# The up projection's rows moved by 64 bytes inside their tiles

## The chip, the cores and the metric

The kernel runs on one core of a Trainium2 chip. The metric is the device time of one execution in microseconds: 1368.78 us as the median of three runs before the change. Instructions run on TensorE (PE in the rows; its weight loads are PEld), VectorE (DVE), ScalarE (ACT), GpSimd (POOL) and SyncE (SP), which issues most transfers.

## The reference

Two transformer-like blocks follow each other on 256 tokens of width 1024. The last step of the second block is a mixture of 16,384 tiny experts, and the change touches its second half alone:

```python
def block(args):
    xb, ib, gb = args
    u = w_down[ib]
    act = jax.nn.gelu(jnp.einsum("td,thkd->thk", xb, u), approximate=False) * gb
    v = w_up[ib]
    return jnp.einsum("thk,thkd->td", act, v)
...
return rmsnorm_2(h, norm_final_w)[:, N_META:]
```

Each token takes 8 x 16 experts. The result of the block is added to the stream, and the sum is normed.

## The kernel before, in words

The kernel computes the expert layer densely: for every expert and every token an activation, times a gate that is zero where the token did not choose the expert. The 16,384 experts are 128 rows of 128. The down projection (tile `S`, lines 222 to 224) makes for each row `i` a tile of 128 experts x 256 tokens, `AT`; the up projection multiplies row `i`'s activations with the 128 x 1024 matrix `wu[i]` and adds into four banks of PSUM, `acc[t][f]`, for two halves `t` of the tokens and two halves `f` of the 1024 outputs.

Every product in the kernel is done in two parts for precision. `load_split` (from line 198) loads a 128 x 1024 piece of weights as `wf` (four buffers), ACT casts it to the reduced form `wh` (line 217), and DVE subtracts, `wl = wf - wh` (line 218). The other operand is split in the same way, and three multiplications, high x high, high x low and low x high, take the place of one. In the up projection the function `up_row` (from line 1499) multiplies the row with its gates on DVE (line 1507) and then splits it into `ah` (ACT, line 348) and `al` (DVE, line 349), each 128 x 256 words. Row 0 and row 1 are made earlier (`UP_EARLY`); the rows up to 95 use the pool `gp` and its tags `oh` and `og`, whose slots are as large as the gate tiles of the same tags, 512 words a partition, two of each; from row 96 on a pool `up` with four of each takes their place, in the space that the tile `AT0` of 96 rows leaves.

The inner loop is `products`. Here the row is the stationary operand (128 of its 256 columns, loaded into TensorE by a weight load before every multiplication) and `wu`'s part is the moving one, 512 columns at a time. A row has 2 x 3 x 2 = 12 multiplications, and the 128 rows 1536, in program order; the last three rows do their second half of the tokens at the end. TensorE takes its instructions in the order of the program; loads run ahead on SP's queue as far as the four `wf` buffers allow, and the splits follow them on ACT and DVE.

Where the tiles lie. A tile's place is counted in bytes from a partition's start. `wf`, `wh` and `wl` are 4096 bytes, the slots of `gp` 2048, `AT0` 96 x 1024, the slots of `up` 1024, and `S`'s moving tiles `xth` and `xtl` 8 x 272 words: all are multiples of 256, and in the built program `wh`, `wl`, `ah`, `al`, `xuh` and `xul` all begin 32 bytes past a multiple of 256. So do all slices of `acc`'s operands, which are cut at multiples of 512 bytes. "Distance" below is the moving operand's address minus the stationary operand's, modulo 256. In `acc` it is 0. In the queries' product `q` (moving `xuh`, `xul`, 256 columns) it is 0 as well. In the second feed-forward product (moving `fah`, `fal`, 256 columns), whose tiles lie 224 past a multiple of 256, it is 192 throughout. In `S` (moving `xth`, `xtl`, 256 columns, rows of 272 words) it is 64 x `k` for the eight steps `k`, three multiplications each. The kernel's first projection, `tma` (512 columns) and `tmb` (262 columns), has weights as the moving operand and rows of 272 words as the stationary one, so its distance at step `k` is -64 x `k`: 0 at `k` = 0 and 4, 192 at 1 and 5, 128 at 2 and 6, 64 at 3 and 7.

Of the kernel before, what the change touches and what calls it, by code (L numbers as in the profile page):

```python
# [8 lines left out]
F32R = mybir.dt.float32r  # L9
# [7 lines left out]
P = 128  # L17
T = 256
# [51 lines left out]
LN_WAIT = 1.5, 3.0  # L70

LAST = 3

UP_EARLY = 2

# [83 lines left out]
def tile_two_blocks(ctx: ExitStack, tc: tile.TileContext, A, out):  # L159
# [172 lines left out]
    def pin(ins):  # L332
        tc.keep_in_program_order(ins)
# [11 lines left out]
    def split_to(dh, dl, src, scale=None):  # L345

        if scale is None:
            nc.scalar.copy(dh, src)  # L348
            nc.vector.tensor_sub(dl, src, dh)  # L349
        else:  # L350
            nc.scalar.activation(dh, src, AF.Copy, scale=scale)
            nc.vector.scalar_tensor_tensor(dl, src, scale, dh, op0=OP.mult, op1=OP.subtract)
# [197 lines left out]
    oh = ap.tile([P, 8, T], F32R, name="oh")  # L550
# [298 lines left out]
    for g in range(9):  # L849
# [21 lines left out]
        if g >= 1:  # L871
            ah, al = held[g - 1]
# [356 lines left out]
    for step in ORDER.split():  # L1229
# [28 lines left out]
        elif kind == "w":  # L1258
# [6 lines left out]
            oh, ol = (och, ready["ocl"]) if g >= 8 else pairs[g // 4]  # L1265
            i = g - 8 if g >= 8 else g % 4
# [185 lines left out]
    def at_rows(a, b):  # L1452
        for lo, hi, t in parts:
            x, y = max(a, lo), min(b, hi)
            if x < y:
                yield x, y, t[:, x - lo:y - lo, :]
# [42 lines left out]
    def up_row(i, up):  # L1499

        (_, _, r), = list(at_rows(i, i + 1))
        r = r[:, 0, :]
        n = max(x for x in gts if x <= i)
        gt = gts[n][:, :min(P - n, gts[n].shape[1]), :]
        if i == n and i >= 7:
            pin(nc.sync.dma_start(gt, G0r[:, i:i + gt.shape[1], :]))
        pin(nc.vector.tensor_mul(r[:, :P], r[:, :P], gt[:, i - n, :]))
        ah = up.tile([P, T], F32R, tag="oh", name=f"ah{i}")
        al = up.tile([P, T], F32R, tag="og", name=f"al{i}")
        if i < UP_EARLY:  # L1510
            pin(nc.scalar.copy(ah, r))
            pin(nc.vector.tensor_sub(al, r, ah))
        else:
            split_to(ah, al, r)
        up_rows[i] = (ah, al)

    for i in range(0, P, 2):
        if i == P - 2:

            bg.drain()  # L1520
            for n in (0, 3, 5):
                nc.gpsimd.dma_start(gts[n], G0r[:, n:n + gts[n].shape[1], :])
            for j in range(UP_EARLY):
                up_row(j, gp)
        S = bank(f"S{i}").rearrange("p (a t) -> p a t", a=2)
        for e in range(2):
            wh, wl = load_split(A["wd"][i + e], [P, 8, P])
            for k in range(8):
                mm3(S[:, e, :], wh[:, k, :], wl[:, k, :], xth[:, k, :], xtl[:, k, :], k == 0 and e == 0, k == 7)
            bg.run(BUDGET["select"] if state["toks"] == P else BUDGET["down"])  # L1530
        n = state["toks"]
        rs = list(at_rows(i, i + 2)) if len(parts) > 1 or i < NA else []
        assert len(rs) == 1
        r = rs[0][2]
        if n == P:
            nc.scalar.activation(r, S, AF.Gelu)
        else:
            nc.scalar.activation(r[:, :, :P], S[:, :, :P], AF.Gelu)
            if n < T:
                nc.scalar.activation(r[:, :, n:], S[:, :, n:], AF.Gelu)  # L1540
            g = stage[(i // 2) % 2].rearrange("p (a t) -> p a t", a=2)
            nc.scalar.activation(g[:, :, P:n], S[:, :, P:n], AF.Gelu)
            nc.vector.tensor_mul(r[:, :, P:n], r[:, :, P:n], g[:, :, P:n])
        state["rows"] = i + 2
# [6 lines left out]
    up = gp  # L1551
    for i in range(P):
        if i == NA:

            sat.close()
            up = sp.enter_context(tc.tile_pool(name="up", bufs=4))
        if i == NB:
            pin(nc.scalar.activation(first, first, AF.Sqrt))
        if i not in up_rows:
            up_row(i, up)  # L1560
        ah, al = up_rows.pop(i)
        wh, wl = load_split(A["wu"][i], [P, D])

        def products(t, fs, i=i, ah=ah, al=al, wh=wh, wl=wl):
            c = slice(t * P, (t + 1) * P)
            for l, w, e in ((ah, wh, False), (ah, wl, False), (al, wh, i == P - 1)):
                for f in fs:
                    nc.tensor.matmul(acc[t][f], l[:, c], w[:, f * 512:(f + 1) * 512], start=False, stop=e,  # L1568
                                     skip_group_check=True)

        products(0, (0, 1))
        if i >= P - LAST:
            late.append(products)
        else:
            products(1, (0, 1))
# [109 lines left out]
```

## Time and profile before

| | |
|---|---|
| timed runs | 1365.6, 1368.78 and 1371.24 us |
| profiled execution | 1370.11 us, its span 1368.4 us |
| TensorE busy | 1350.3 us, 99% of the span |
| DVE, ACT, POOL busy | 985.9, 756.3, 307.1 us |
| mean granted clock of TensorE | 0.992 of 2.4 GHz |
| first and last start of a multiplication into `acc` (line 1568) | 1014.3 and 1362.3 us |

The span runs from the first to the last instruction of one profiled execution; the execution's own time holds the start and the end around it too. Matmuls are pipelined and their ends are modelled, so the records of two overlap: what a multiplication costs is read from one start to the next and not from its own length.

### The profile page before, as it was taken

To read this page: it belongs to the slowest core of one execution; us is meant where nothing else is said; L and a number is where in the kernel's file an instruction comes from. 1 tells how busy PE (TensorE), PEld (TensorE's weight loads), DVE (VectorE), ACT (ScalarE), POOL (GpSimd) and SP (SyncE) were. 2 spreads that over 40 slices of the span, in tenths; PEclk is the share of its full clock that TensorE was granted. 3 is DMA by queue.
4 is the path that set the end of the run, shared out by engine and by line. 5 is a ranking of instruction groups with operands and counts; after the bars stand their busy time and mean duration, and the time that the engine had idled before them with its cause. 6 is when DMAs were issued, how large, how long until landed. Compare 5 with 4: busy or idle time off the path is not lost.

```text
span 1368.4 us, 25834 instructions
## 1 busy us (share of the span) xinstructions
PE 1350.3 (99%) x10054; PEld 1255.6 (92%) x10054; DVE 985.9 (72%) x1924; ACT 756.3 (55%) x1263; POOL 307.1 (22%) x223
## 2 busy tenths in 40 slices
PE   9999999999999999999999999999999999999998
PEld 8988899999888899999999999999998888888886
DVE  6985777657637896798989976666666666666665
ACT  6665444445334675654544548787755555555454
POOL 3122200000310000000048888888600000000000
PEclk9999999999999999999999999999999999999999
DMA  8466666663663343645668776666666777677764
GB/s 297 141 220 226 185 185 189 194 189 113 202 195 107 108 141 109 200 143 165 185 184 186 186 186 156 159 151 158 172 201 220 212 224 220 216 218 214 221 210 131
DMA packets 120730, 250.45 MB, mean 183 GB/s; under 512 B 28048, under 2 KB 52368, under 8 KB 120480
## 3 DMA queue, kind: packets, MB, share of 16 engines
q1 hardware_dynamic: 97328, 235.89, 56.3%
q0 software_dynamic: 22704, 12.35, 6.3%
q8 instruction: 79, 1.29, 0.4%
q10 hardware_dynamic: 576, 0.57, 0.1%
q14 instruction: 43, 0.35, 0.1%
HBM read 234.60 MB, written 9.50 MB: 178 GB/s over the span
## 4 chain that ended last, share of the span: by engine, by line
PE 93%; DVE 3%; DMA 2%; ACT 1%; issue 1%; POOL 0%; SPq 0%; DVEq 0%; ACTq 0%; POOLq 0%
PE acc L1568 25%; PE S L224 9%; PE S L223 9%; PE S L222 9%; PE ff L222 4%; PE ff L223 4%; PE ff L224 4%; PE pg L1476 2%; PE cv L922 2%; PE wo L222 2%; PE wo L224 2%; PE wo L223 2%; PE cf L222 1%; PE cf L224 1%; PE cf L223 1%; PE q L223 1%
## 5 line engine op out<-in xcount | busy, mean ns | idle before, releaser
L218 DVE TENSOR_TENSOR wl<-wf,wh 128x1024 fp32r<-128x1024 f32 (+1 forms) x425 | 515.7, 1215 | 234.7 <-ACT wh L217 234.1
L217 ACT CAST wh<-wf 128x1024 fp32r<-128x1024 f32 (+1 forms) x425 | 442.8, 1043 | 377.9 <-PE S L223 145.4
L222 PE MATMUL S<-xth,wh 128*128 128x256 f32 x1024 | 289.6, 283 | 0.0
L223 PE MATMUL S<-xtl,wh 128*128 128x256 f32 x1024 | 288.6, 282 | 0.0
L224 PE MATMUL S<-xth,wl 128*128 128x256 f32 x1024 | 288.3, 282 | 0.0
L1350 POOL DMA_INDIRECT G<-small x128 | 241.9, 1890 | 163.4 <-DVE small L1344 124.7
L224 PEld LDWEIGHTS S<-xth,wl 128*128 128x128 f32 x1024 | 194.2, 190 | 0.0
L222 PEld LDWEIGHTS S<-xth,wh 128*128 128x128 f32 x1024 | 193.8, 189 | 0.0
L223 PEld LDWEIGHTS S<-xtl,wh 128*128 128x128 f32 x1024 | 192.5, 188 | 0.0
L1568 PE MATMUL acc<-wh,ah 128*128 128x512 f32 x512 | 158.3, 389 | 0.0
L1568 PE MATMUL acc<-wl,ah 128*128 128x512 f32 x512 | 158.2, 389 | 0.0
L1568 PE MATMUL acc<-wh,al 128*128 128x512 f32 x512 | 158.1, 389 | 0.0
L348 ACT CAST ah<-AT 128x256 fp32r<-128x256 f32 x126 | 50.9, 404 | 116.4 <-DVE wl L218 114.3
L1568 PEld LDWEIGHTS acc<-wl,ah 128*128 128x128 f32 x512 | 96.2, 188 | 19.9
L1568 PEld LDWEIGHTS acc<-wh,al 128*128 128x128 f32 x512 | 96.2, 188 | 19.8
L1568 PEld LDWEIGHTS acc<-wh,ah 128*128 128x128 f32 x512 | 96.1, 188 | 19.8
L222 PE MATMUL ff<-h2h,wh 128*128 128x256 f32 x256 | 73.1, 287 | 1.0 <-ACT wh L217 0.6
L222 PE MATMUL ff<-fah,wh 128*128 128x256 f32 x256 | 71.3, 280 | 1.7 <-ACT fah L348 1.7
L223 PE MATMUL ff<-h2l,wh 128*128 128x256 f32 x256 | 72.7, 284 | 0.0
L223 PE MATMUL ff<-fal,wh 128*128 128x256 f32 x256 | 71.6, 280 | 1.1 <-DVE fal L349 1.1
L224 PE MATMUL ff<-h2h,wl 128*128 128x256 f32 x256 | 72.2, 284 | 0.4 <-DVE wl L218 0.4
L349 DVE TENSOR_TENSOR al<-AT,ah 128x256 fp32r<-128x256 f32 x126 | 53.4, 424 | 26.2 <-ACT ah L348 26.2
(501 smaller groups left out, 2691.6 us busy)
## 6 DMA issues: line engine op xcount, KB each, us to landing
wf<-in_wd_dram SPq DMA_DIRECT2D x128, 512.0 KB, 3.7
wf<-in_wu_dram SPq DMA_DIRECT2D x128, 512.0 KB, 3.6
wf<-in_w_ff_dram SPq DMA_DIRECT2D x64, 512.0 KB, 4.2
wf<-in_w_out_dram SPq DMA_DIRECT2D x24, 512.0 KB, 3.6
G<-zg POOLq DMA_DIRECT2D x16, 512.0 KB
wf<-in_w_conf_dram SPq DMA_DIRECT2D x16, 512.0 KB, 3.8
wf<-in_w_xbc_dram SPq DMA_DIRECT2D x16, 512.0 KB, 5.0
wf<-in_w_q_dram SPq DMA_DIRECT2D x16, 512.0 KB, 3.7
```

The lines of the kernel that those rows point to most:

```text
L217: nc.scalar.copy(wh[:, :n], wf[:, :n])
L218: nc.vector.tensor_sub(wl[:, :n], wf[:, :n], wh[:, :n])
L222: nc.tensor.matmul(o, lh, rh, start=start, stop=False, skip_group_check=True)
L223: nc.tensor.matmul(o, lh, rl, start=False, stop=False, skip_group_check=True)
L224: nc.tensor.matmul(o, ll, rh, start=False, stop=stop, skip_group_check=True)
L348: nc.scalar.copy(dh, src)
L349: nc.vector.tensor_sub(dl, src, dh)
L922: nc.tensor.matmul(pcv[32 * g:32 * g + 32, i, :], taps[:, m, g, q, :], r4[:, i, g, 4 * q:4 * q + T], start=(i == 0 and q == 0), stop=(q == ...
L1350: s = nc.gpsimd.indirect_dma_start(out=G0, out_offset=bass.IndirectOffsetOnAxis(ap=idx[:, c:c + 1], axis=0), in_=gv[:, c:c + 1], in_offset ...
L1476: nc.tensor.matmul(pg[:, i, :], oh[:, i, :], og[:, i, :], start=True, stop=True, skip_group_check=True)
L1568: nc.tensor.matmul(acc[t][f], l[:, c], w[:, f * 512:(f + 1) * 512], start=False, stop=e, skip_group_check=True)
```

## The change

`UP_PHASE` is a constant of 16 words. Both tiles of a row are allocated 64 words longer, and the row lies from word 16 on. `up_row`, `products` and all else are as before.

```diff
+UP_PHASE = 16
...
-        ah = up.tile([P, T], F32R, tag="oh", name=f"ah{i}")
-        al = up.tile([P, T], F32R, tag="og", name=f"al{i}")
+        ah = up.tile([P, T + 64], F32R, tag="oh", name=f"ah{i}")[:, UP_PHASE:UP_PHASE + T]
+        al = up.tile([P, T + 64], F32R, tag="og", name=f"al{i}")[:, UP_PHASE:UP_PHASE + T]
```

## Rows read from the trace of the kernel before

**Rows 1.** The page: busy time by engine; chain that ended last, by engine and line.
```profile
PE 1350.3 (99%) x10054; PEld 1255.6 (92%) x10054; DVE 985.9 (72%) x1924; ACT 756.3 (55%) x1263; POOL 307.1 (22%) x223
...
PE 93%; DVE 3%; DMA 2%; ACT 1%; issue 1%; POOL 0%; SPq 0%; DVEq 0%; ACTq 0%; POOLq 0%
PE acc L1568 25%; PE S L224 9%; PE S L223 9%; PE S L222 9%; PE ff L222 4%; PE ff L223 4%; PE ff L224 4%; PE pg L1476 2%; PE cv L922 2%; PE wo L222 2%; PE wo L224 2%; PE wo L223 2%; PE cf L222 1%; PE cf L224 1%; PE cf L223 1%; PE q L223 1%
```

**Rows 2.** Busy time by engine, two windows of `acc`; then granted clock, DMA.
```profile
1050.00:1100.00 50.00, 50.00 (x222) 41.45 (x221) 33.78 (x56) 27.26 (x37) 0.00 (x0) 1.00 0.72 218
1100.00:1150.00 50.00, 50.00 (x222) 41.42 (x221) 34.37 (x55) 26.29 (x36) 0.00 (x0) 1.00 0.70 216
```

**Rows 3.** Costs by line, then DMA, 1020 to 1360 us (total us, mean ns).
```profile
L218 DVE TENSOR_TENSOR wl<-wf,wh 128x1024 fp32r<-128x1024 f32 x124 | 152.0, 1226 | 84.3 <-ACT wh L217 84.3
L217 ACT CAST wh<-wf 128x1024 fp32r<-128x1024 f32 x124 | 130.6, 1054 | 42.6 <-issue 39.6 <-PE acc L1568 2.7
...
L349 DVE TENSOR_TENSOR al<-AT,ah 128x256 fp32r<-128x256 f32 x125 | 52.9, 423 | 26.2 <-ACT ah L348 26.2
L348 ACT CAST ah<-AT 128x256 fp32r<-128x256 f32 x125 | 50.5, 404 | 115.5 <-DVE wl L218 114.3 <-issue 1.2
L1507 DVE TENSOR_TENSOR AT<-AT,small 128x128 f32<-128x128 f32 x121 | 34.5, 285 | 0.0
...
DMA packets 33328, 71.60 MB, mean 211 GB/s; under 512 B 2432, under 2 KB 17818, under 8 KB 33306
...
wf<-in_wu_dram SPq DMA_DIRECT2D x120, 512.0 KB, 3.6
```

**Rows 4.** Line 1568: durations min/median/max in ns, first and last start.
```profile
L1568 PE MATMUL acc<-wh,ah x512: 389/389/398, 1014.3 to 1361.8; 128*128 128x512 f32 x171
L1568 PEld LDWEIGHTS acc<-wl,ah x512: 187/188/188, 1014.5 to 1361.8; 128*128 128x128 f32 x171
...
L1568 PE MATMUL acc<-wh,al x512: 387/389/393, 1015.2 to 1362.3; 128*128 128x512 f32 x171
```

**Rows 5.** `fah` from 183 us: weight loads; first and last of 94 timeline rows.
```profile
L222 PEld LDWEIGHTS ff<-fah,wh x30: 187/188/188, 182.9 to 192.7; 128*128 128x128 f32 x30
...
182.65 0.28 PE L222 MATMUL ff<-fah,wh 128*128 128x256 f32 x1
...
193.19 0.28 PE L222 MATMUL ff<-fah,wh 128*128 128x256 f32 x1
```

**Rows 6.** `q` from 579 us: weight loads; first and last of 85 timeline rows.
```profile
L222 PEld LDWEIGHTS q<-xuh,wh x28: 192/192/193, 578.8 to 588.5; 128*128 128x128 f32 x28
...
578.42 0.28 PE L224 MATMUL q<-xuh,wl 128*128 128x256 f32 x1
...
588.50 0.28 PE L224 MATMUL q<-xuh,wl 128*128 128x256 f32 x1
```

**Rows 7.** TensorE's timeline at the beginning of `acc`, two multiplications a row.
```profile
1014.31 0.62 PE L1568 MATMUL acc<-wh,ah 128*128 128x512 f32 x2
1014.76 0.63 PE L1568 MATMUL acc<-wl,ah 128*128 128x512 f32 x2
1015.23 0.62 PE L1568 MATMUL acc<-wh,al 128*128 128x512 f32 x2
1015.69 0.62 PE L1568 MATMUL acc<-wh,ah 128*128 128x512 f32 x2
1016.15 0.63 PE L1568 MATMUL acc<-wl,ah 128*128 128x512 f32 x2
1016.62 0.62 PE L1568 MATMUL acc<-wh,al 128*128 128x512 f32 x2
```

**Rows 8.** Timeline of `S`, first and last of 27 rows.
```profile
639.81 0.28 PE L223 MATMUL S<-xtl,wh 128*128 128x256 f32 x1
...
642.89 0.28 PE L222 MATMUL S<-xth,wh 128*128 128x256 f32 x1
```

**Rows 9.** Timeline of `tma`: at `k` = 4, then at `k` = 5.
```profile
15.22 0.40 PE L222 MATMUL tma<-wh,hh 128*128 128x512 f32 x1
...
15.91 0.28 PE L222 MATMUL tmb<-wh,hh 128*128 128x262 f32 x1
...
18.54 0.39 PE L222 MATMUL tma<-wh,hh 128*128 128x512 f32 x1
...
19.24 0.28 PE L222 MATMUL tmb<-wh,hh 128*128 128x262 f32 x1
```

## Prediction

> **What bounds the kernel now.** I read the page's busy shares and chain first: TensorE is busy for 1350.3 of 1368.4 us, the chain that ended last is TensorE for 93%, and its largest single entry is the up projection's multiplications, `acc`, with 25% [rows 1]. The change touches the operands of those alone, so the rest of the reading is of that stage. In its windows TensorE is busy for 50.00 of every 50 us at the full 2.4 GHz level, and DVE and ACT for 34 and 27 [rows 2]. By line, one `acc` row (12 multiplications) costs ACT 1054 + 404 ns = 1.46 us and DVE 1226 + 423 + 285 ns = 1.93 us [rows 3]; from 1014.3 to 1362.3 us there are 1536 multiplications, so 1535 starts follow each other in 348.0 us: 226.7 ns each, 2.72 us a row [rows 4]. The stage is therefore bound by the pace at which TensorE begins one multiplication after another. At 2.4 GHz, 512 columns are 213.3 ns; 13.4 ns are left over each time, 20.5 us in the stage. That is all that a better placed operand could win.
>
> The trace shows that placement can matter. In the second feed-forward product (`fah`, `fal`; the moving rows lie 192 bytes past the weights modulo 256) 93 starts take 193.19 - 182.65 us, 113.3 ns each for 256 columns [rows 5]. In the queries' product (`xuh`, `xul`; distance 0) 84 starts take 588.50 - 578.42 us, 120.0 ns each [rows 6]. 256 columns are 106.7 ns, so 6.7 ns are left over at distance 192 and 13.3 ns at distance 0. The `acc` stage lies at distance 0 and has 13.4 ns left over. The weight loads tell the two states apart too: median 188 ns at distance 192 [rows 5], 192 ns in the queries' product [rows 6].
>
> **The change part by part.** No instruction, transfer or wait is added or removed; four things can differ.
>
> *The tiles.* A row's high and low part take 320 words of their slot in place of 256. The early rows' slots are sized by the 512-word gate tiles; the later pool of eight tiles grows by 8 x 256 bytes a partition within what the 96-row `AT0` tile released. 1280 bytes are again a multiple of 256, so every row gets the new distance. Cost 0; nothing waits for that space.
>
> *The writers.* ACT's cast (404 ns) and DVE's subtraction (423 ns) write 64 bytes further on [rows 3]. The trace has no row for one operand moved by 64 bytes, so by the nearest rows a change lies between nothing and, as an upper end, the whole duration again: 1.86 us on ACT, 2.35 on DVE. Both stay below TensorE's 2.72 us a row and are hidden; I take 0. Were that cover gone, 0.4 us x 128 rows would be 51 us.
>
> *The loads of weights from HBM.* 211 GB/s move in the stage and a transfer lands 3.6 us after its issue, while four buffers cover 4 x 2.72 us [rows 3]. A stage 3% quicker does not reach that. Cost 0.
>
> *The start-to-start time of the 1536 multiplications.* Here the moving operand is the 512-column weight and the stationary one the row, so the 64 bytes make moving minus stationary 192. Everything hangs on what the 13.4 ns are. Two readings fit the settled states. In the first they are a conflict of one weight load with the stream and fall from 13.3 to 6.7 ns, whatever the length of the stream. In the second a stream itself loses 1/16 of its columns' time (6.7 ns in 256, 13.3 in 512), and the conflict comes on top: 0 in `fah`, 6.7 ns in the queries, 0 in `acc`. Three rows speak for the second. (a) The weight load in `acc` takes 188 ns, as in `fah` and not as in the queries [rows 4 to 6]. (b) The first ten `acc` starts, before the rhythm settles, take 1016.62 - 1014.31 us, 231.0 ns each, 17.7 over; the down projection's `S`, whose distance changes after every three multiplications and which never settles, takes 26 starts in 642.89 - 639.81 us, 118.5 ns, 11.8 over [rows 7, 8]. The gap of 5.9 ns between 512 and 256 columns is near the second reading's 6.7 and far from the first's 0. (c) The only other 512-column stream, `tma`, has, at the very distance 192 that the change makes, three starts in 19.24 - 18.54 us, 233 ns, and at distance 0 three in 15.91 - 15.22 us, 230 ns [rows 9]. None is near 220. Against them: those three are short runs between 262-column ones, and `fah` needs some multiplications to settle as well.
>
> So the price of one multiplication at distance 192 has the ends 220.0 ns (first reading: 213.3 + 6.7) and 233.3 ns (second reading with the queries' conflict: 226.7 + 6.7; the `tma` row is as high). That is -6.7 to +6.6 ns, times 1535: -10.2 to +10.2 us. I take 0: by (a) the stage is already in the state without conflict, and a weight load of 188 ns ends 39 ns before the next one begins, 226.7 ns after it [rows 4], while at 113 or 120 ns two are always under way: beside 512 columns a load can be late at no cost.
>
> The Trainium skill, "TensorE: Matmul & The Clock Gate", section "Step-by-step: what each phase is for", says that TensorE has two independent read ports, so that loading the next weights takes nothing from the running multiplication. By that rule distance never matters and the time stays. The 113.3 against 120.0 ns of rows 5 and 6 contradict it as stated. The same page, section "Wait — 56ns, not 53.3ns?", gives columns over 2.4 GHz plus about 2.5 ns as the pace, 215.8 ns here; a change that reached that would save an estimated 16.7 us, and no row of this trace comes near it.
>
> **The sum.** The profiled execution took 1370.1 us, 1.7 more than its span; 1370.1 + 0 = 1370.1. It lies 1.3 us above the median of the three timed runs, 1368.8, to which the forecast refers: 1369 us. Its own range is 1364 to 1374: the spread of those runs (1365.6 to 1371.2) and 2 ns either way on 1535 starts, 3 us.
>
> **The rivals.** *Faster: the conflict reading is right.* Each start falls to 220.0 ns, 10.2 us less, 1358.6. For it: 13.3 ns at distance 0 is left over in both the queries and `acc`, and 6.7 at 192. Against it: (a), (b), (c).
>
> *Slower: the settled rhythm is lost.* `acc` at distance 0 settles after ten starts and stays settled to the end. At distance 192 a 512-column stream may settle with a conflict or not at all, as `S` does not. Unsettled, it costs 231.0 ns [rows 7], 4.3 x 1535 = 6.6 us, 1375.4; with the queries' conflict, or as in the `tma` row of distance 192, 233.3, 10.2 us, 1379.0. It decides from a mean of 231.2 ns on (4.45 ns x 1535 = 6.8 us). For it: (c), and that the distance which settles without conflict is 192 for 256 columns but evidently 0 for 512, so it need not be both. Against it: loads that are late have room beside 512 columns.
>
> *The rows do not get the distance.* If slots began elsewhere modulo 256, nothing would change but the arithmetic of addresses; the slot sizes above exclude that, and it would give 1369 too.
>
> **How the numbers follow.** No change, the rows' not getting the distance included, 0.46; faster 0.22; slower 0.32. What a measurement of this kernel can tell from no change is about 0.5%, 6.8 us. The faster rival lies wholly beyond that. Of the slower one about an eighth (0.04) is a half-settled state within it. So faster 0.22, same 0.50, slower 0.28. Leaving out either rival would leave out more than 0.2, so the range takes in both ends: 1358 to 1380.
>
> **What would show it.** Right: starts of `acc` 226 to 227 ns apart after a short beginning, weight loads at 188 ns, the stage from its first to its last start 348 us long, all earlier stages unchanged. The first rival: 220 ns apart, the stage 338 us. The second: 229 to 234 ns, changing from one to the next, or even 233, weight loads of 190 to 192 ns in part, the stage 355 to 358 us. The prediction is wrong in its main step if the mean of the settled starts is below 224 or above 230 ns, and wrong in its cover if TensorE shows idle time in the stage.

## Result: slower by half a per cent, all of it in the up projection's stage

| | before | after |
|---|---|---|
| median of 5 timed runs (lowest to highest), us | 1368.78 (1364.86 to 1371.24) | 1375.58 (1373.79 to 1377.91) |
| profiled execution / its span, us | 1370.11 / 1368.4 | 1375.58 / 1373.9 |
| first start of `acc`, us | 1014.3 | 1009.6 |
| start to start in `acc`, ns | 226.7 | 233.3 |
| weight load in `acc`, median ns | 188 | 188 |

The ratio of the two kernels' mean times is 1.0056, with a 95% interval from 1.0033 to 1.008: slower by 4.5 to 11.0 us. The medians differ by 6.8 us. The forecast was 1369 us in a range of 1358 to 1380. The time lies in the range because the range took in both rivals; what came is the mechanism of the slower rival and not the likeliest case.

The page of the kernel after: busy time by engine, then the chain that ended last. The number of multiplications is the one of [rows 1]; the chain's largest entry, `acc`, has grown from 25% to 26%.

```profile
PE 1355.6 (99%) x10054; PEld 1251.3 (91%) x10054; DVE 986.2 (72%) x1924; ACT 756.4 (55%) x1263; POOL 306.0 (22%) x223
...
PE 92%; DVE 3%; DMA 2%; ACT 2%; issue 1%; POOL 0%; SPq 0%; ACTq 0%; DVEq 0%; POOLq 0%
PE acc L1570 26%; PE S L226 9%; PE S L225 9%; PE S L224 9%; PE ff L225 4%; PE ff L226 4%; PE ff L224 4%; PE pg L1478 2%; PE cv L924 2%; PE wo L224 2%; PE wo L226 2%; PE wo L225 2%; PE cf L224 1%; PE cf L226 1%; PE cf L225 1%; PE q L225 1%
```

Two windows of the stage after, the same stretches as [rows 2]: TensorE has no idle time and the full clock in both kernels, yet it begins 216 multiplications in 50 us and not 222. DVE and ACT are less busy because fewer rows go through.

```profile
1050.00:1100.00 50.00, 50.00 (x216) 40.30 (x215) 33.35 (x54) 25.80 (x37) 0.00 (x0) 1.00 0.67 210
1100.00:1150.00 50.00, 50.00 (x216) 40.30 (x215) 33.04 (x54) 25.80 (x37) 0.00 (x0) 1.00 0.69 213
```

The line of the multiplications after, as in [rows 4]: duration min/median/max in ns, then the first and the last start of each form. From the first start to the last, 1009.6 to 1367.8, are 1535 starts: 358.2 us, 233.3 ns each, against 348.0 us and 226.7 ns before. That is 10.2 us more, while the weight load still takes 188 ns. The order of the last rows makes the last `wh,ah` start the 1533rd after the first, so its row alone gives the pace as well: 357.7 / 1533 = 233.3. I use that row for the experiments below.

```profile
L1570 PE MATMUL acc<-wh,ah x512: 393/398/398, 1009.6 to 1367.3; 128*128 128x512 f32 x171
...
L1570 PEld LDWEIGHTS acc<-wl,ah x512: 188/188/188, 1009.9 to 1367.3; 128*128 128x128 f32 x171
...
L1570 PE MATMUL acc<-wh,al x512: 393/395/398, 1010.6 to 1367.8; 128*128 128x512 f32 x171
```

The timeline of TensorE after, two multiplications a row: six starts in 1101.55 - 1100.15 us are 233.3 ns each, in turn 231 and 236, and the pace is this from the stage's beginning to its end.

```profile
1100.15 0.63 PE L1570 MATMUL acc<-wh,al 128*128 128x512 f32 x2
1100.62 0.63 PE L1570 MATMUL acc<-wh,ah 128*128 128x512 f32 x2
1101.09 0.63 PE L1570 MATMUL acc<-wl,ah 128*128 128x512 f32 x2
1101.55 0.63 PE L1570 MATMUL acc<-wh,al 128*128 128x512 f32 x2
```

That ACT and DVE write the rows 64 bytes further on is not the reason. The last row is written by 1362.51 us (1362.09 + 0.42), and the multiplications behind that keep the slower pace: 17 starts in 1367.78 - 1363.82 us, 232.9 ns each as far as two decimals tell.

```profile
1362.09 0.42 DVE L351 TENSOR_TENSOR al<-AT,ah 128x256 fp32r<-128x256 f32 x1
...
1363.82 0.39 PE L1570 MATMUL acc<-wh,ah 128*128 128x512 f32 x1
...
1367.78 0.40 PE L1570 MATMUL acc<-wh,al 128*128 128x512 f32 x1
```

**Why the total moved by less than the stage.** The stage cost 10.2 us more, but the profiled execution is only 5.5 us longer, because `acc` began 4.7 us earlier. So did `S` already, at 616.8 us and not 621.5, and the change touches no multiplication ahead of `acc`. What differs there is TensorE's granted clock. These are windows of 50 us of the kernel before; the third figure from the end is the granted clock, 1.00 for 2.4 GHz.

```profile
100.00:150.00 50.00, 46.77 (x355) 43.90 (x354) 32.17 (x63) 28.33 (x50) 15.04 (x25) 0.93 0.71 225
...
300.00:350.00 50.00, 48.19 (x378) 47.38 (x377) 30.42 (x52) 24.09 (x39) 0.96 (x3) 0.93 0.48 140
...
450.00:500.00 50.00, 47.42 (x377) 44.55 (x376) 46.09 (x79) 34.70 (x65) 1.01 (x1) 0.97 0.36 108
```

And the same windows of the kernel after:

```profile
100.00:150.00 50.00, 45.94 (x371) 43.03 (x370) 32.48 (x63) 28.94 (x53) 15.06 (x25) 1.00 0.74 231
...
300.00:350.00 50.00, 48.97 (x390) 47.50 (x389) 31.44 (x57) 25.34 (x40) 2.09 (x6) 0.97 0.47 143
...
450.00:500.00 50.00, 47.42 (x391) 44.62 (x390) 46.14 (x76) 36.71 (x73) 1.01 (x1) 1.00 0.40 125
```

Before, four stretches of the first 600 us (6.8, 3.4, 6.8 and 3.4 us) ran at the lower level, 1.2 GHz, 20.5 us in all; after, 6.8 us in all. All these windows have some idle time of TensorE in them, but such a window does not always lose clock: from 450 to 500 us TensorE is busy for 47.42 us in both kernels, at 0.97 and at 1.00. In eleven profiles of kernels whose multiplications are the same up to `acc`, its start goes with the time at the lower level: 3.4 us gave 1007.8 and 1008.4, 6.8 gave 1008.3 and 1009.6, 10.2 gave 1009.7, 1010.8 and 1011.1, 20.5 gave 1013.1 to 1014.3. It changes from one execution to the next by up to 6.5 us, about the spread of the five runs of before (6.4 us). The total times agree. Of the 20 executions of the kernel before that ran beside the experiments, on three chips, those with a mean granted clock of 0.997 or 0.998 took 1363.2 to 1365.1 us, those with 0.994 or 0.995 took 1365.8 to 1368.4, and those with 0.991 or 0.992 took 1368.6 to 1370.9. At 0.997 the kernel after took 1375.3 and 1375.6 us against 1365.1, at 0.998 it took 1373.8 against 1363.2 to 1364.3: at the same clock it is 9.5 to 10.6 us slower, as its stage says. No experiment set the clock, so that the clock causes the spread is an inference from these agreements. The difference of the medians, 6.8 us, is then 10.2 us of the stage blurred by it; 10.2 lies inside the interval. The stage's own start-to-start time is the sharper measure, and the experiments are read by it.

### The profile page after: what moved, and what is told of

Read it like the earlier page. It is cut to its first block, busy times and chain, and to the rows that moved or that the text cites. A ratio compares the mean times of both kernels' runs of the same rounds, so it can differ in the third digit from the quotient of the medians.

```text
span 1373.9 us, 25834 instructions
## 1 busy us (share of the span) xinstructions
PE 1355.6 (99%) x10054; PEld 1251.3 (91%) x10054; DVE 986.2 (72%) x1924; ACT 756.4 (55%) x1263; POOL 306.0 (22%) x223
## 4 chain that ended last, share of the span: by engine, by line
PE 92%; DVE 3%; DMA 2%; ACT 2%; issue 1%; POOL 0%; SPq 0%; ACTq 0%; DVEq 0%; POOLq 0%
PE acc L1570 26%; PE S L226 9%; PE S L225 9%; PE S L224 9%; PE ff L225 4%; PE ff L226 4%; PE ff L224 4%; PE pg L1478 2%; PE cv L924 2%; PE wo L224 2%; PE wo L226 2%; PE wo L225 2%; PE cf L224 1%; PE cf L226 1%; PE cf L225 1%; PE q L225 1%
## 5 line engine op out<-in xcount | busy, mean ns | idle before, releaser
L1570 PE MATMUL acc<-wh,ah 128*128 128x512 f32 x512 | 161.5, 396 | 0.0
L1570 PE MATMUL acc<-wh,al 128*128 128x512 f32 x512 | 161.5, 395 | 0.0
L1570 PE MATMUL acc<-wl,ah 128*128 128x512 f32 x512 | 161.4, 396 | 0.0
```

## Experiments

The letters that the expectations use: theory A says that the distance sets the pace of `acc`; rival B, that it is the longer tiles; C, that any row not at the beginning of its tile costs the same; D, that it is the row's own address modulo 256; E, that ACT or DVE take over as the limit; F, that a stream has more than one pace that keeps itself up and that its beginning decides. R1 and R2 are the prediction's two readings of the 13.4 ns: a loss of fixed size that depends on the distance, and 1/16 of the stream's time with a conflict on top. A rhythm is a pattern of start-to-start times that repeats. The kernel before took 1367.09 us beside experiments 1 to 3 (one execution), 1366.37 beside 4 to 6 (median of 8) and 1368.83 beside 7 to 9 (median of 11). Each time below is that of a single execution where no median is named.

### 1. The longer tiles without the shift

The kernel after, with the row at the beginning of its longer tile.

```
-UP_PHASE = 16
+UP_PHASE = 0
```

> The rows' tiles are 64 words longer, but the row lies at word 0: distance 0 as before. Theory A (the distance between the moving weights and the row, modulo 256, sets the pace): acc starts 226.7 ns apart, stage 348 us from first to last start. Rival B (the longer tiles or the other slots of the later pool cost the time): 233.3 ns, 358 us.

The row of its multiplications: 347.5 / 1533 = 226.7 ns, as before. 1365.44 us.

```profile
L1570 PE MATMUL acc<-wh,ah x512: 389/389/397, 1009.7 to 1357.2; 128*128 128x512 f32 x171
```

Rival B falls: the tiles' length costs nothing, and what costs 10.2 us is the shift by 64 bytes alone.

### 2. Shifts by 32 and by 48 words

In the kernel after: distance 128, and, with 48 in the place of 32, distance 64.

```
-UP_PHASE = 16
+UP_PHASE = 32
```

> The row lies at word 32 of its tile: distance 128. Theory A gives this distance a pace of its own, between 226.7 and 233.3 ns, and not necessarily one number for every start. Rival C (any row that is not at the start of its tile costs the same): 233.3 ns again. If a start takes under 226 ns here, 226.7 is not the least that a stream of 512 columns can take.

> The row lies at word 48 of its tile: distance 64. As for distance 128: theory A gives a pace of its own between 226.7 and 233.3 ns, rival C 233.3 ns; under 226 ns would show that 226.7 is not the least for 512 columns.

With 32 words: 356.2 / 1533 = 232.4 ns on average, and start to start between 228 and 241 ns in a rhythm of several steps; 1375.28 us.

```profile
L1570 PE MATMUL acc<-wh,ah x512: 388/393/405, 1010.8 to 1367.0; 128*128 128x512 f32 x171
```

With 48 words: 357.7 / 1533 = 233.3 ns, even (233, 233, 234); the weight load takes 189 ns; 1379.42 us.

```profile
L1570 PE MATMUL acc<-wh,ah x512: 397/397/400, 1013.5 to 1371.2; 128*128 128x512 f32 x171
L1570 PEld LDWEIGHTS acc<-wl,ah x512: 189/189/189, 1013.7 to 1371.2; 128*128 128x128 f32 x171
```

All three distances other than 0 cost 5.7 to 6.6 ns a multiplication. With 512 columns, 0 is the best of the four; only multiples of 64 bytes were tried. Rival C gave the 233.3 ns at 48 words, but not the 232.4 at 32; the next run bears on it too.

### 3. Both operands moved alike

In the kernel before, sixteen words at the beginning of the constants' pool push every tile behind them by 64 bytes, rows and weights alike: the row's own address changes, the distance stays 0.

```
+    cpool.tile([P, 16], F32, name="pad16")
```

> A tile of 16 words is put ahead of all others, so that every tile of the kernel before moves by 64 bytes: rows and weights both lie 96 past a multiple of 256, and all distances are as before. Theory A: acc 226.7 ns a start, 348 us, and the rest as before. Rival D (the row's own address counts, 96 in place of 32): 233.3 ns, 358 us.

347.5 / 1533 = 226.7 ns; 1363.29 us.

```profile
L1569 PE MATMUL acc<-wh,ah x512: 389/389/397, 1007.5 to 1355.0; 128*128 128x512 f32 x171
```

Rival D falls: with its address moved by the same 64 bytes as in the change, the row costs nothing as long as the weights move too. That speaks against C as well. It is the difference of the two addresses that counts. The Trainium skill, "TensorE: Matmul & The Clock Gate", section "Step-by-step: what each phase is for", says that TensorE has two independent read ports, so that loading the next weights takes no read bandwidth from the running multiplication. Runs 1 to 3 do not fit that as stated, since nothing but the place of one operand against the other changes between 226.7 and 233.3 ns; where in TensorE or in the memory the two meet, no run shows.

### 4. The same work in streams of 256 columns, at distance 192

The kernel after, with every multiplication cut in two.

```
-                    nc.tensor.matmul(acc[t][f], l[:, c], w[:, f * 512:(f + 1) * 512], start=False, stop=e,
-                                     skip_group_check=True)
+                    for q in range(2):
+                        nc.tensor.matmul(acc[t][f][:, q * 256:(q + 1) * 256], l[:, c],
+                                         w[:, f * 512 + q * 256:f * 512 + (q + 1) * 256], start=False, stop=e,
+                                         skip_group_check=True)
```

> The changed kernel, but each multiplication of 512 moving columns in the up projection is cut into two of 256: 3072 multiplications at distance 192. Theory A (pace set by distance and by length together, the settled distance being 192 for 256 columns and 0 for 512): 113.3 ns a start, 348 us for the stage, as long as before the change although the operands lie as in the changed kernel. Rival D (the row's new place is bad by itself): 116.7 ns or more, 358 us or more.

The stage took 362.0 us from the first of 3072 starts to the last, 117.9 ns each, not the 113.3 of `fah` [rows 5]; 1378.08 us. Only the last 39, after a wait of TensorE for `wl`, ran faster, as the timeline's last rows show (two multiplications a row): 26 starts in 1370.29 - 1367.34 us, 113.5 ns each.

```profile
L1571 PE MATMUL acc<-wh,ah x1024: 276/281/281, 1008.4 to 1369.9; 128*128 128x256 f32 x171
```

```profile
1367.34 0.39 PE L1571 MATMUL acc<-wl,ah 128*128 128x256 f32 x2
...
1370.29 0.39 PE L1571 MATMUL acc<-wh,al 128*128 128x256 f32 x2
```

The expectation of 113.3 was missed, and 117.9 lies above the 116.7 from which on rival D was to count; but run 3 had excluded D, and the last 39 starts reach 113.5 ns at the same addresses. Distance 192 allows two rhythms with 256 columns, and each keeps itself up; the distance does not decide alone there.

### 5. A quarter of the weight load

Stationary operand 32 of 128 columns wide, so that a weight load is shorter, at distance 0 in the kernel before and at 192 in the kernel after. Three quarters of the product are left out.

```
-                    nc.tensor.matmul(acc[t][f], l[:, c], w[:, f * 512:(f + 1) * 512], start=False, stop=e,
+                    nc.tensor.matmul(acc[t][f][:32], l[:, c.start:c.start + 32], w[:, f * 512:(f + 1) * 512], start=False, stop=e,
```

> The kernel before, but the up projection uses 32 of the 128 tokens of each stationary operand (three quarters of the product are left out), so that a weight load brings 32 columns in place of 128, at distance 0. Theory R2 (the stream itself loses 1/16 of its columns' time, 13.3 ns in 512, and the settled state has no conflict): 226.7 ns a start still. Rival R1 (the 13.3 ns are a conflict of the weight load with the stream): a quarter of it, 216 to 218 ns.

> The changed kernel, but with stationary operands of 32 columns, at distance 192. R2 with a conflict of 6.7 ns on top: the 226.7 ns of the stream and at most a quarter of the conflict, 226.7 to 228.4 ns. R1: the whole 20 ns left over are the weight load's and fall to a quarter, 218 ns. If 233.3 ns remain, the length of the weight load has no part in the loss.

At distance 0: loads of 108 ns and not 188, and yet 355.1 / 1533 = 231.6 ns a multiplication, in a pattern from 229 to 235; 1371.73 us.

```profile
L1568 PE MATMUL acc<-wh,ah x512: 391/394/398, 1008.3 to 1363.4; 128*32 128x512 f32 x171
L1568 PEld LDWEIGHTS acc<-wl,ah x512: 107/108/112, 1008.5 to 1363.4; 128*32 128x32 f32 x171
```

At distance 192: 355.2 / 1533 = 231.7 ns; 1376.53 us.

```profile
L1570 PE MATMUL acc<-wh,ah x512: 390/394/397, 1013.1 to 1368.3; 128*32 128x512 f32 x171
```

Both readings missed at distance 0 (216 to 218 ns by R1, 226.7 by R2), and both at 192 (218 by R1, 226.7 to 228.4 by R2): with the shorter load the pace is worse at distance 0 and better at 192, and the two no longer differ. The run does not separate the load's duration from the narrower operand. It does show that the loss does not simply follow the load's duration, which is therefore no measure of it.

### 6. The down projection's `S` moved to distance 192

In the kernel before. The rows that `S` and others take as one operand (in `S` the moving one) become a view that can begin 48 words into its tile, with rows of 256 and not 272 words, so that the distance is 192 at all eight steps; here only those of `S`.

```
+PHASED = ("xt",)
...
-        h = act.tile([P, 8, TM], F32R, name=f"{name}h", tag="acth")
-        l = act.tile([P, 8, TM], F32R, name=f"{name}l", tag="actl")
-        return h[:, :, :t], l[:, :, :t]
+        h = act.tile([P, 8 * TM], F32R, name=f"{name}h", tag="acth")
+        l = act.tile([P, 8 * TM], F32R, name=f"{name}l", tag="actl")
+        if name in PHASED:
+            return [x[:, 48:48 + 8 * T].rearrange("p (k t) -> p k t", k=8) for x in (h, l)]
+        return [x.rearrange("p (k t) -> p k t", k=8)[:, :, :t] for x in (h, l)]
```

> The kernel before (up projection at distance 0), but the down projection's moving operand lies 192 bytes past the weights for all eight steps (rows of 256 words, 48 words into the tile). Theory A: S settles at 113.3 ns where it has 118 to 120 now; some 2950 starts in a row times 5 ns are 15 us less, about 1354 us. Rival E (ACT or DVE, busy 73% and 68 to 91% in that stage, take over): a part of it, down to nothing, with TensorE idle in the stage.

Median of 5: 1361.46 us against 1366.37; the ratio of the runs is 0.9955 [0.9936, 0.9975]. The 15 us of theory A were missed. `S` went from a mean of 118.3 to 117.1 ns, some 3.8 us over its 3038 starts in a row: the first 1726 have the slower rhythm throughout, and only 466 of the 3038 follow at 113 or 114 ns. The timeline of this kernel shows both in one execution: 18 starts in 641.89 - 639.77 us are 117.8 ns each, 29 starts in 843.89 - 840.61 us are 113.1 ns each.

```profile
639.77 0.28 PE L226 MATMUL S<-xth,wl 128*128 128x256 f32 x1
...
641.89 0.28 PE L226 MATMUL S<-xth,wl 128*128 128x256 f32 x1
...
840.61 0.28 PE L225 MATMUL S<-xtl,wh 128*128 128x256 f32 x1
...
843.89 0.28 PE L224 MATMUL S<-xth,wh 128*128 128x256 f32 x1
```

In `S` the rhythm changes where another multiplication (`pg`) comes between, and not elsewhere.

### 7. Does the way in decide the pace of 512 columns too?

The kernel after, with one to five small multiplications into a bank of their own ahead of every eighth row: 15 interruptions. In full precision each of them stands in the timeline as two.

```
+        if i and i % 8 == 0:
+            kick = bank(f"kick{i}")
+            for _ in range((i // 8 - 1) % 5 + 1):
+                nc.tensor.matmul(kick[:, :P], ident, ident, start=True, stop=True, skip_group_check=True)
```

> The changed kernel (distance 192), but before every eighth row one to five short multiplications in full precision into a bank of their own interrupt the stream, 15 times, so that its rhythm starts again from another moment. Theory A (distance and length alone decide where a stream settles): after each interruption it comes back to 233.3 ns. Theory F (a stream has more than one rhythm that keeps itself, and the entry decides, as the 256-column S showed at distance 192 with 113.3 and 117.9): after some interruptions it stays at another pace, down to 226.7, and the stage is shorter than 358 us plus the interruptions.

After each of the 15 the mean was 233.30 to 233.34 ns, alternating (231, 236) or even (233), never 226.7; the wait at the interruption itself is not counted in it. The timeline around the first: 12 starts in 1035.54 - 1032.74 us before it, 14 in 1039.96 - 1036.69 us behind it, 233.3 and 233.6 ns each. The time, 1389.58 us, has the interruptions in it.

```profile
1032.74 0.63 PE L1574 MATMUL acc<-wh,al 128*128 128x512 f32 x2
...
1035.54 0.62 PE L1574 MATMUL acc<-wh,al 128*128 128x512 f32 x2
1036.00 0.38 PE L1568 MATMUL kick<-cst 128*128 128x128 f32 x2
1036.14 0.72 PE L1574 MATMUL acc<-wh,ah 128*128 128x512 f32 x2
1036.69 0.63 PE L1574 MATMUL acc<-wl,ah 128*128 128x512 f32 x2
...
1039.96 0.39 PE L1574 MATMUL acc<-wh,al 128*128 128x512 f32 x1
```

With 512 columns the distance decides after all 15 ways in, and theory F falls for them: the alternating and the even rhythm have the same mean.

### 8. Streams of 384 columns at both distances

In the kernel before and in the kernel after; a quarter of the product is left out.

```
-                    nc.tensor.matmul(acc[t][f], l[:, c], w[:, f * 512:(f + 1) * 512], start=False, stop=e,
+                    nc.tensor.matmul(acc[t][f][:, :384], l[:, c], w[:, f * 512:f * 512 + 384], start=False, stop=e,
```

> The kernel before (distance 0), but each multiplication of the up projection takes 384 of the 512 columns (a quarter of the product is left out). R2 (a stream loses 1/16 of its columns' time at least): no settled state under 170.0 ns (160.0 + 10.0). A fixed loss for each multiplication: 173.3 ns with the 13.3 ns of 512 columns, or 166.7 with the 6.7 ns that 256 columns can reach; a pace under 169 ns refutes R2.

> The changed kernel (distance 192) with 384 of the 512 columns. R2: 170.0 ns or above; with the conflict of 6.7 ns that 512 columns have at this distance 176.7. A fixed loss of 6.7 ns: 166.7 ns, which would refute R2.

At distance 0: 266.0 / 1533 = 173.5 ns, even; 1282.3 us.

```profile
L1568 PE MATMUL acc<-wh,ah x512: 334/334/338, 1007.8 to 1273.8; 128*128 128x384 f32 x171
```

At distance 192: 268.1 / 1533 = 174.9 ns, changing between 170 and 178; 1287.59 us.

```profile
L1570 PE MATMUL acc<-wh,ah x512: 332/336/340, 1011.1 to 1279.2; 128*128 128x384 f32 x171
```

With the other lengths, the time of a multiplication beyond columns / 2.4 GHz, in ns:

| columns | distance 0 | distance 192 |
|---|---|---|
| 256 | 13.3 [rows 6] | 6.7 [rows 5] or 11.2 (run 4) |
| 384 | 13.5 | 14.9 |
| 512 | 13.4 [rows 4] | 20.0 |

At distance 0 the loss is the same at all three lengths; at 192 it grows with the length, and the two cross between 256 and 384. R1's fixed 6.7 ns at distance 192 is refuted. R2's floor of 1/16 of the stream is not contradicted (no rhythm that holds is below 113.3, 170 or 226.7 ns), but not shown either: 384 columns at distance 0 stay 3.5 ns above it.

### 9. The larger 256-column products at 192, the up projection at 0

Run 6 with two more names, and the queries' rows in the same manner; the up projection as before. `h2` are the rows of the first feed-forward product; `h` are those of the first block's projections, the products `qk` and `u` of 256 columns. `tma` and `tmb` take `h` as stationary operand, so their distance becomes 64 at every step. The smaller 256-column products stay where they were.

```
-PHASED = ("xt",)
+PHASED = ("xt", "h2", "h")
...
-    xuh = qp.tile([P, 8, T], F32R, name="xuh")
-    xul = qp.tile([P, 8, T], F32R, name="xul")
+    xuh, xul = [qp.tile([P, 8 * T + 64], F32R, name=n)[:, 48:48 + 8 * T].rearrange("p (k t) -> p k t", k=8)
+                for n in ("xuh", "xul")]
```

> The kernel before with the up projection at distance 0, and with distance 192 for the down projection, the first feed-forward product, the queries' product and the first block's projections from the normed input (all of 256 columns). By the paces that the trace of before shows for settled 256 columns (113.3 against 118 to 120), if all of them settle there: S as in the kernel with S alone or up to 15 us less than before, the first feed-forward product some 3 us less, the queries 2 us, the projections 1 us; 1345 to 1362 us. If the entry decides (theory F): the gain of S alone (5 us) and part of the rest, 1357 to 1362.

1351.11 us, median of 6 (1349.79 to 1360.56), against 1368.83: ratio of the runs 0.9899 [0.987, 0.9928]. It lies in the expected 1345 to 1362 and beats both kernels. The line of `S` before, then those of `S` and `acc` in this run's profile:

```profile
L222 PE MATMUL S<-xth,wh x1024: 276/280/367, 621.5 to 1013.9; 128*128 128x256 f32 x171
...
L224 PE MATMUL S<-xth,wh x1024: 276/276/369, 613.8 to 993.7; 128*128 128x256 f32 x171
...
L1572 PE MATMUL acc<-wh,ah x512: 389/389/396, 994.1 to 1341.6; 128*128 128x512 f32 x171
```

So the part ahead of `S` gave 7.7 us: 768 multiplications of the first feed-forward product by 4.0 ns (a mean of 117.6 to 113.6), 3.1 us; 384 of the queries by 2.8 (119.8 to 117.0), 1.1 us; 192 of `qk` and 72 of `u` by 4.1 and 4.3 ns, 1.1 us. The 2.4 us that remain are not the placement: TensorE spent 10.2 us ahead of `acc` at the lower clock and not 20.5, which moved the start of `acc` by 2.0 to 4.6 us in the profiles above. `S` took 379.9 us in place of 392.4, 12.5 less (mean 114.2 ns), and `acc` has its 226.7 ns (347.5 / 1533). Together 20.2 of the 20.3 us between the two profiled executions, 1370.11 and 1349.82, of which 17.8 are the products' paces; the medians differ by 17.7. In the queries, of constant distance in both kernels, the move from 0 to 192 alone gave the 2.8 ns; in `S` the distance also stopped changing from step to step, and no run separates the two. `S` began in the faster rhythm here, at the same distance as in run 6: 19 starts in 641.93 - 639.78 us, 113.2 ns each.

```profile
639.78 0.28 PE L224 MATMUL S<-xth,wh 128*128 128x256 f32 x1
...
641.93 0.28 PE L225 MATMUL S<-xtl,wh 128*128 128x256 f32 x1
```

Four of its six runs lie between 1349.8 and 1352.3 us, two at 1359.0 and 1360.6; that these two fell into the slower rhythm in `S` fits the size, but they have no trace, so this is argued and not shown.

## Why the prediction's main step failed

**The tiles, the writers, the loads from HBM: right.** Taken at 0, and 0 by run 1 for the tiles (226.7 ns, 1365.44 us). For the writers, in the stage after, DVE's subtraction still takes 424 ns (423 in [rows 3]); in the windows above TensorE had no idle time, so the cover held.

```profile
L351 DVE TENSOR_TENSOR al<-AT,ah 128x256 fp32r<-128x256 f32 x122 | 51.8, 424 | 33.4 <-ACT ah L350 33.4
```

**The start-to-start time: wrong.** This is the step that failed. Of the price at distance 192, from 220.0 to 233.3 ns, I took 226.7, no change. It measured 233.3, the upper end to a tenth: +6.65 ns x 1535 = +10.2 us.

- Argument (a) carried the choice: a weight load of 188 ns in `acc` as in `fah`, not 192 as in the queries, was to mean a state without conflict. After the change the load still takes 188 ns and the pace is 6.6 ns worse; in run 5 it takes 108 ns and the pace is 231.6 and 231.7. In these runs the duration of a load says nothing of what it costs the stream.
- The consequence drawn from it, that beside 512 columns a load can be late at no cost because it ends 39 ns before the next, falls with it. Run 5 had some 80 ns more room and lost 5 ns.
- Argument (c) pointed the right way: the three starts of `tma` at distance 192, 233 ns, and at distance 0, 230 ns [rows 9], came from the only product of before with this length at this distance. I put them behind (a) because they are short runs. That 233 is also the pace that came is in part luck: the other three starts at `k` = 4, distance 0 too, take 16.98 - 16.27 us, 237 ns each, where `acc` settles at 226.7. Three starts between shorter ones do not give a pace to a few ns.

```profile
16.27 0.40 PE L222 MATMUL tma<-wh,hh 128*128 128x512 f32 x1
...
16.98 0.28 PE L222 MATMUL tmb<-wh,hh 128*128 128x262 f32 x1
```

- Argument (b), that the loss grows with the length, holds at distance 192 and not at distance 0 (run 8). The prediction looked for one law for both.

**The rivals.** *Slower* came, as a pace of its own and not as unsettled starts: 233.3 ns in alternating pairs of 231 and 236, its upper price. Its point of decision, 231.2 ns, was passed; its sign in the weight loads, 190 to 192 ns in part, did not come. The total it names for this pace, 1379.0 us, is 3.4 above the median, which fits the higher clock of the executions after the change (0.996 to 0.998). *Faster* read the 6.7 ns of 256 columns into 512; the 233.3 ns and run 8 refute it, and run 4 shows that even for 256 columns the 6.7 are one of two prices at that distance. *The rows do not get the distance* is excluded by the changed pace.

**The size of the total.** The own range, 1364 to 1374, allowed 2 ns either way on the starts, where they moved by 6.65. That the median still came within 1.6 us of it is luck: the part ahead of `acc` moves by up to 6.5 us from one execution to the next, and the executions after the change fell on its short side.

What stays open: what makes the loss depend on the distance, why it is the same for all lengths at distance 0 and grows at 192, why the narrower stationary operand costs more at distance 0, and whether 17/16 of the stream's time is a floor. No run here separates these.

## What to carry to other kernels

Where TensorE never idles, read the start-to-start time of its multiplications for each length of stream and each distance (moving minus stationary address) in the trace, and take the price of a new combination from long runs of the same length and distance, not from the duration of the weight load or from another length. Even such a row can be one of two rhythms: `fah` had 113.3 ns, and run 4 at the same length and distance 117.9. So try the placement, and read the new pace. Here streams of 256 columns did best at 192 bytes, of 0 and 192 (64 and 128 were not tried for all steps alike), and streams of 512 at 0: leaving 0 cost the 512-column stage 10.2 us, and moving the larger 256-column products to 192 gave 17.7 us in the median. Where the total moves with the granted clock from run to run, judge such a change by its stage.

## What the runs showed of the hardware

- The pace of a multiplication with a weight load each depends on the two operands' addresses against each other: 512 columns took 226.7 ns at distance 0, 233.3 at 64, 232.4 at 128, 233.3 at 192. Moving both alike changes nothing (run 3).
- With 256 columns at distance 192 there are two rhythms, 113 and 118 ns, that each hold for hundreds of starts; in `S` they change only at interruptions (runs 4, 6, 9). With 512 columns an interruption does not change the mean (run 7).
- A weight load of 32 columns lasts 108 ns in place of 188, yet the 512-column stream at distance 0 is slower with it, 231.6 against 226.7 ns; at distance 192 it takes 231.7, so the two no longer differ (run 5).
- Stretches at 1.2 GHz of 3.4 or 6.8 us come in different places and numbers in executions of the same instructions, 3.4 to 20.5 us in all, and the start of `acc` lay with them between 1007.8 and 1014.3 us.
